# Regrouping the projections, the attention and its filler in a hybrid encoder block

## The chip, the cores and the metric

The kernel runs on one core of a Trainium2 chip. The metric is the device time of one launch in microseconds (us), lower is better. The kernel before takes 1700.06 us, the median of three runs (1698.44 to 1700.27).

## The reference

One residual block on x of 1024 rows (T) by 1024 channels. A normed x is multiplied by one wide input matrix, whose columns feed three token mixers and three merge gates. Then follow one output projection and a ConvGLU channel mixer.

```python
h = _rmsnorm(x, norm_mix_g); z = h @ w_in
(hq, hf, hi, hg, fq, fk, fv, ff, mq, gate_logits) = split(z)
y_a = _hgrn2_mixer(hq, hf, hi, hg, ...)      # gated linear recurrence, 4 heads, 128 x 128 state
y_b = _fox_mixer(fq, fk, fv, ff, ...)        # forgetting attention, 8 heads of 64, causal
y_c = _memory_mixer(mq, mem_kv, ...)         # cross-attention into 256 memory tokens, 4 heads of 128
gates = sigmoid(gate_logits)                 # 3 x 1024 channels
merged = sum(gates[b] * (y_b @ w_br[b]) for the three branches)
x = x + merged @ w_out
x = x + conv_glu_ffn(_rmsnorm(x, norm_ffn_g))

# inside _fox_mixer, for each block of 128 queries lo:hi
s = (q[lo:hi] @ k[:hi].T) * scale + Fc[lo:hi] - Fc[:hi]       # Fc: running sum of log-forget
p = softmax(where(causal, s, -inf)); out = p @ v[:hi]
```

## The kernel before

Every large product is done in three parts. Each fp32 operand is split into a rounded high part (ScalarE cast, L166) and the rest (VectorE subtraction, L174), and `mm3` (L160 to L162) issues high x high, high x low and low x high into one accumulation bank. On the profile these are the three lines with most of TensorE's time.

The instructions are not issued in the order of the program's text alone. A scheduler places them on each engine's queue by a simulated time and by priority; `ahead(gen, AHEAD)` raises the priority of a generator's steps, `weave` alternates the steps of several generators in given proportions, and `tc.issue_after(ins)` puts an order on one engine: what is built inside stands behind `ins` on its queue, with no wait for its end. `held` (in the recurrence) uses this to spread filler.

The stages, in order of time:

- The start loads x, makes high and low parts of x^T (`uh`, `ul`, in eight chunks of 128 channels) and does the first two gates and the memory tokens' keys and values.
- The dense stage (`dense_unit`) does the four chunks of the cross-attention's queries and ten gate chunks in pairs, each pair with seven block products in place of eight (Winograd's form of Strassen's scheme): 7 x 4 x 3 matmuls for two chunks of 128 output channels. Its weights come on GpSimd's DMA queue. A chunk done directly (`cm_chunk`) takes 8 k-chunks x 2 halves x 3 matmuls of 512 columns.
- `fox_values` (values and forget logits) and `fox_proj(0)` make the attention's inputs token by token: in `token_major` the stationary operand is a 128-token block of `uh` or `ul`, and 256 (or 264) columns of weights move through. The cross-attention (`memory`) runs between them.
- The attention goes by pairs of heads. `fox_prep(p)` transposes a pair's normed queries and keys and makes `kh`, `kl`, `qa`. `fox_attn(p, i)` goes through one head: two query blocks get logits (L924, L925), bias and row maximum (L930), exp (L940), reciprocal (L941) and scaling on GpSimd (L942); then the scaled blocks are transposed (L953 to L956), split, and multiplied with the values (L965, L966), 256 columns at a time. The next two query blocks follow.
- Between those steps TensorE gets other work, the filler: in a pair's first head the next pair's projection, in its second head three gate chunks (`gates_early`); in the last pair the recurrence's values (`hgrn_values`) and one gate. `fox_prep(p + 1)` stands between the two heads of pair p, behind the last logits.
- The recurrence (`hgrn_prep`, `hgrn_mix`), with the next head's preparation as filler, then the three branch projections, the output projection, the ConvGLU up products (the same seven-product scheme) and the down products.

Names that the text uses: `Vf` holds the attention's values and later the recurrence's; `rt` and `rx` are the norm of a row, by token and spread; `gd`, `mqd`, `ybd`, `ycd` are DRAM scratch; `raw`, `wh`, `wl` are a weight tile and its two parts.

Of the kernel before, what the change touches and what calls it, by code (L numbers as in the profile page):

```python
# [14 lines left out]
P = 128  # L15
# [13 lines left out]
NCOVER, NPAIR = 2, 10  # L29
NDULL = 8  # L30
NFOX = [0, 3, 0, 3, 0, 3, 1]
# [3 lines left out]
assert 2 + NCOVER + NPAIR + sum(NFOX) == len(ORDER) and len(_dense) % 2 == 0  # L35
# [3 lines left out]
FOX_STEPS, HGRN_STEPS, MEM_STEPS = 28, 14, 7  # L39
AHEAD = 300  # L40
FOX_LATE = 0.2
# [68 lines left out]
def tile_block(ctx: ExitStack, tc: tile.TileContext, xT, memT, x_rows, mem_rows, vec, fbias, mats, hmask, w_first, w_cm, w_hi, w_fqk, w_fv,  # L110
# [77 lines left out]
    def weights(src, shape, raw=None, hl=None, parts=1):  # L188
# [4 lines left out]
        if hl is None:  # L193
            hl = [wp.tile([P, 4 * 264], F32R, tag=t, name=t, bufs=3) for t in ("wh", "wl")]
# [227 lines left out]
    def first_weights(k):  # L422
        k0, k1 = WFIRST[k]
        if k % 4 == 0:
            gw[k // 4] = [wp.tile([P, 4 * 264], F32R, tag=t, name=t, bufs=3) for t in ("wh", "wl")]
        sl = slice((k0 % 4) * 256, (k1 - 1) % 4 * 256 + 256)
        split(S, gw[k // 4][0][:, sl], gw[k // 4][1][:, sl], wg[k // 4][:, sl])
# [124 lines left out]
    def product(ps, op, b, first):  # L552
        wh, wl = op
        for k in range(4):
            ks = slice(k * P, (k + 1) * P)
            bh, bl = block(b, k)
            mm3(ps, wh[:, ks], wl[:, ks], bh, bl, first and k == 0, k == 3, not first)

    class Dense:
# [16 lines left out]
        def operand(self, src):  # L576
            if self.half is None:
                self.half = [wp.tile([P, 4 * 264], F32R, tag=t, name=t, bufs=3) for t in ("wh", "wl")]
# [125 lines left out]
    def token_major(src, ncol, evac):  # L704

        with tc.issue_after(late["load"].ins):
            w = [weights(src[q], (4, ncol)) for q in range(2)]
        for tb in range(8):
            ps = ps_proj()[:, :ncol]
            tsl = slice(tb * P, (tb + 1) * P)  # L710
            for k in range(KC):
                wh, wl = w[k // 4]
                mm3(ps, uh[k][:, tsl], ul[k][:, tsl], wh[:, k % 4, :], wl[:, k % 4, :], k == 0, k == KC - 1)
# [130 lines left out]
    def fox_proj(p):  # L844

        fox_z[p] = [None, None]

        def evac(tb, ps):
            n, b = tb // 4, tb % 4
            if b == 0:  # L850
                fox_z[p][n] = pq.tile([P, 4, 256], F32, tag="z", name=f"z{p}_{n}", bufs=2)
            z = fox_z[p][n]
            S.activation(z[:, b, :], ps, AF.Copy, scale=rt[:, tb:tb + 1])
            if b == 3:
                zz = z.rearrange("p b (h d) -> p (b h) d", d=64)
                sq = pools["pf"].tile([P, 16, 64], F32, tag="pt", name="fsq", bufs=4) if p else \
                    pm.tile([P, 16, 64], F32, tag="fsq", name="fsq")
                r = cp.tile([P, 16], F32, tag="fr", name="fr", bufs=2)
                S.activation(sq, zz, AF.Square)
                V.reduce_sum(r, sq, axis=AX.X)  # L860
                rstd_small(r, r, 64)
                V.tensor_mul(zz, zz, r.unsqueeze(2).to_broadcast([P, 16, 64]))

        yield from token_major(w_fqk[p], 256, evac)

    def fox_prep(p, after=None):
# [3 lines left out]
        for n in range(2):  # L870
            sl = slice(n * HB, (n + 1) * HB)
            z = fox_z[p][n]
            for what in range(2):
                gc = col(C_FK) if what == 0 else fqs
                ptr = ps_tr()
                with tc.issue_after(after.ins) if after is not None else nullcontext():
                    for b in range(4):
                        PE.transpose(ptr[:, b * P:(b + 1) * P], z[:, b, what * P:(what + 1) * P], ident)
# [13 lines left out]
        fox_sets[p] = [kh, kl, qa, None]  # L892
# [7 lines left out]

    def fox_attn(p, i):
        kh, kl, qa, _ = fox_sets[p]
# [7 lines left out]
        for tp in range(4):  # L910
            pts = []
            for j in range(2):
                tb = 2 * tp + j
                ns = (tb + 1) * P
                tsl = slice(tb * P, (tb + 1) * P)
                pt = pf.tile([P, T], F32, tag="pt", name="pt", bufs=4)
# [4 lines left out]
                for s0 in range(0, ns, HB):  # L921
# [3 lines left out]
                    fox_sets[p][3] = PE.matmul(ps[:, :w], qa[i][:, tsl], kl[i][:, s0:s0 + w], start=False, stop=True)  # L925
# [14 lines left out]
                S.activation(pt[:, :ns], pt[:, :ns], AF.Exp, bias=st[:, 2:3], accum_out=st[:, 3:4])  # L940
                V.reciprocal(st[:, 3:4], st[:, 3:4])  # L941
                G.tensor_scalar(pt[:, :ns], pt[:, :ns], st[:, 3:4], 0.0, ALU.mult, ALU.add)  # L942
                pts.append(pt)
                yield
            po = ps_po()
            for sp in range(tp + 1):
                ptr = ps_tr()
                w = 384 if sp == tp else 512
                for jj in range(2):
                    sb = 2 * sp + jj  # L950
                    ssl = slice(sb * P, (sb + 1) * P)
                    if sb <= 2 * tp:
                        PE.transpose(ptr[:, jj * 256:jj * 256 + P], pts[0][:, ssl], ident)  # L953
                        PE.transpose(ptr[:, jj * 256 + P:jj * 256 + 256], pts[1][:, ssl], ident)
                    else:
                        PE.transpose(ptr[:, 256:384], pts[1][:, ssl], ident)  # L956
                ph = pf.tile([P, HB], F32R, tag="ph", name="ph", bufs=2)
                pl = pf.tile([P, HB], F32R, tag="pl", name="pl", bufs=2)
                split(S, ph[:, :w], pl[:, :w], ptr[:, :w])
                for jj in range(2):  # L960
                    sb = 2 * sp + jj
                    last = sb == 2 * tp + 1
                    o = po[:, P:256] if last else po[:, 0:256]
                    src = slice(256, 384) if last else slice(jj * 256, jj * 256 + 256)
                    PE.matmul(o, vhl[:, sb, :], ph[:, src], start=(sb == 0), stop=False)  # L965
                    PE.matmul(o, vhl[:, sb, :], pl[:, src], start=False, stop=last)  # L966
# [848 lines left out]
```

## Time and profile before

| | |
|---|---|
| runs | 1698.44, 1700.06, 1700.27 us, median 1700.06 |
| profiled execution | 1700.23 us, its span 1698.4 us |
| TensorE matmul busy | 1691.0 us, 8957 instructions |
| VectorE, ScalarE, GpSimd busy | 1150.8, 800.9, 324.6 us |
| TensorE clock granted, mean | 0.999 |
| DMA moved | 227.16 MB, mean 134 GB/s |

A row of an instruction group reads: line, engine, operation, tiles written and read, shape, count, then busy time in us, mean ns of one, and idle time before them with what ended it. A row of a window reads: start and end, then the busy us of each engine with its count of instructions, granted clock, share of the DMA engines, GB/s. In a list by time the first two numbers are start and duration in us. Ends of matmuls are modelled and overlap the next one.

### The profile page before, as it was taken

To read this page: it belongs to the slowest core of one execution; us is meant where nothing else is said; L and a number is where in the kernel's file an instruction comes from. 1 tells how busy PE (TensorE), PEld (TensorE's weight loads), DVE (VectorE), ACT (ScalarE), POOL (GpSimd) and SP (SyncE) were. 2 spreads that over 40 slices of the span, in tenths; PEclk is the share of its full clock that TensorE was granted. 3 is DMA by queue.
4 is the path that set the end of the run, shared out by engine and by line. 5 is a ranking of instruction groups with operands and counts; after the bars stand their busy time and mean duration, and the time that the engine had idled before them with its cause. 6 is when DMAs were issued, how large, how long until landed. Compare 5 with 4: busy or idle time off the path is not lost.

```text
span 1698.4 us, 24291 instructions
## 1 busy us (share of the span) xinstructions
PE 1691.0 (100%) x8957; PEld 1452.4 (86%) x8957; DVE 1150.8 (68%) x2057; ACT 800.9 (47%) x1428; POOL 324.6 (19%) x420
## 2 busy tenths in 40 slices
PE   9999999999999999999999999999999999999999
PEld 7888899989898998888888888888888888888887
DVE  6966455666666664886856845987878888775654
ACT  6734455545454553775631333644434444533432
POOL 0200032543433331544310000311111111100000
PEclk9999999999999999999999999999999999999999
DMA  9443232221212111110346542566544344494772
GB/s 367 157 161 106 88 139 68 77 92 51 94 59 77 63 46 57 67 32 13 106 127 209 167 186 100 165 174 169 158 139 138 118 149 143 172 363 145 251 269 87
DMA packets 83062, 227.16 MB, mean 134 GB/s; under 512 B 9712, under 2 KB 12408, under 8 KB 82816
## 3 DMA queue, kind: packets, MB, share of 16 engines
q1 hardware_dynamic: 64320, 160.54, 26.8%
q0 software_dynamic: 18048, 64.50, 13.2%
q8 instruction: 70, 1.15, 0.3%
q10 hardware_dynamic: 576, 0.59, 0.1%
q14 instruction: 48, 0.39, 0.1%
HBM read 180.72 MB, written 67.93 MB: 146 GB/s over the span
## 4 chain that ended last, share of the span: by engine, by line
PE 99%; DVE 0%; ACT 0%; DMA 0%; issue 0%; ACTq 0%; DVEq 0%
PE pp L160 21%; PE pp L162 21%; PE pp L161 21%; PE lg L160 4%; PE lg L162 4%; PE lg L161 4%; PE tr L162 3%; PE tr L161 3%; PE tr L160 3%; PE po L966 1%; PE lg L925 1%; PE lg L924 1%; PE po L965 1%; PE po L160 1%; PE po L161 1%; PE po L162 1%
## 5 line engine op out<-in xcount | busy, mean ns | idle before, releaser
L160 PE MATMUL pp<-uh,wh 128*128 128x512 f32 x412 | 163.3, 396 | 0.0
L161 PE MATMUL pp<-ul,wh 128*128 128x512 f32 x412 | 162.9, 395 | 0.0
L162 PE MATMUL pp<-uh,wl 128*128 128x512 f32 x412 | 162.5, 394 | 0.0
L161 PE MATMUL pp<-wl,uh 128*128 128x256 f32 (+1 forms) x512 | 146.3, 286 | 0.0
L162 PE MATMUL pp<-wh,ul 128*128 128x256 f32 (+1 forms) x512 | 146.1, 286 | 0.0
L160 PE MATMUL pp<-wh,uh 128*128 128x256 f32 (+1 forms) x512 | 145.6, 286 | 0.0
L166 ACT CAST wh<-s 128x512 fp32r<-128x512 f32 x110 | 66.5, 621 | 131.6 <-PE pp L161 55.1
L166 ACT CAST wh<-raw 128x1024 fp32r<-128x1024 f32 (+2 forms) x76 | 67.6, 890 | 100.6 <-PE pp L161 86.2
L166 ACT CAST wh<-rw 128x512 fp32r<-128x512 f32 x87 | 53.2, 619 | 108.1 <-PE pp L161 70.2
L160 PEld LDWEIGHTS pp<-wh,uh 128*128 128x128 f32 x512 | 97.3, 190 | 1.2
L161 PEld LDWEIGHTS pp<-wl,uh 128*128 128x128 f32 x512 | 97.4, 190 | 1.0
L162 PEld LDWEIGHTS pp<-wh,ul 128*128 128x128 f32 x512 | 97.4, 190 | 0.9
L1457 POOL DMA_DIRECT2D rw<-in_w_up x44 | 24.1, 555 | 372.4 <-DVE wl L1350 171.3
L166 ACT CAST dwh<-wr 128x1024 fp32r<-128x1024 f32 (+1 forms) x41 | 40.2, 980 | 115.8 <-PE tr L161 40.0
L162 PEld LDWEIGHTS pp<-uh,wl 128*128 128x128 f32 x412 | 77.5, 188 | 15.1
L174 DVE TENSOR_TENSOR wl<-raw,wh 128x1024 fp32r<-128x1024 f32 (+2 forms) x75 | 78.0, 1040 | 17.8 <-ACT wh L166 17.6
L160 PEld LDWEIGHTS pp<-uh,wh 128*128 128x128 f32 x412 | 77.5, 188 | 14.6
L161 PEld LDWEIGHTS pp<-ul,wh 128*128 128x128 f32 x412 | 77.5, 188 | 14.5
L940 ACT ACTIVATE pt<-pt,st 128x128 f32<-128x128 f32 (+3 forms) x64 | 49.7, 777 | 41.7 <-DVE st L937 33.9
L174 DVE TENSOR_TENSOR dwl<-wr,dwh 128x1024 fp32r<-128x1024 f32 (+1 forms) x41 | 46.3, 1129 | 31.7 <-ACT dwh L166 31.7
L942 POOL TENSOR_SCALAR pt<-pt,st 128x128 f32<-128x128 f32 (+3 forms) x64 | 49.1, 767 | 78.4 <-DVE st L941 64.1
L1350 DVE TENSOR_TENSOR wl<-rw,wh 128x512 fp32r<-128x512 f32 x69 | 47.7, 704 | 22.7 <-PE pp L162 18.2
(500 smaller groups left out, 5123.2 us busy)
## 6 DMA issues: line engine op xcount, KB each, us to landing
rw<-in_w_up POOLq DMA_DIRECT2D x44, 512.0 KB, 4.7
sd<-in_w_dn POOLq DMA_DIRECT2D x30, 512.0 KB, 6.0
br<-yd SPq DMA_DIRECT2D x30, 512.0 KB, 5.0
raw<-in_w_cm SPq DMA_DIRECT2D x24, 512.0 KB, 3.4
gd<-gt SPq DMA_DIRECT2D x48, 256.0 KB, 2.0
gt<-gd SPq DMA_DIRECT2D x48, 256.0 KB, 2.7
yd<-fc SPq DMA_DIRECT2D x44, 256.0 KB, 2.2
wr<-sd SPq DMA_DIRECT2D x20, 512.0 KB, 4.5
```

Source lines behind the costliest of these rows:

```text
L160: PE.matmul(ps, lh, rh, start=first, stop=False, skip_group_check=more)
L161: PE.matmul(ps, lh, rl, start=False, stop=False, skip_group_check=more)
L162: return PE.matmul(ps, ll, rh, start=False, stop=last, skip_group_check=more)
L166: return S.copy(out, in_)
L174: return (sub or V).tensor_sub(l, src, h.bitcast(F32))
L924: PE.matmul(ps[:, :w], qa[i][:, tsl], kh[i][:, s0:s0 + w], start=True, stop=False)
L925: fox_sets[p][3] = PE.matmul(ps[:, :w], qa[i][:, tsl], kl[i][:, s0:s0 + w], start=False, stop=True)
L940: S.activation(pt[:, :ns], pt[:, :ns], AF.Exp, bias=st[:, 2:3], accum_out=st[:, 3:4])
L942: G.tensor_scalar(pt[:, :ns], pt[:, :ns], st[:, 3:4], 0.0, ALU.mult, ALU.add)
L965: PE.matmul(o, vhl[:, sb, :], ph[:, src], start=(sb == 0), stop=False)
L1350: late["split"] = V.tensor_sub(l, src, h.bitcast(F32))
L1457: late["raw"] = G.dma_start(raw[:, 2 * i:2 * i + 2, :], src[:, 2 * i:2 * i + 2, :])
```

## The change

- Four more gate chunks go to the dense stage (`NPAIR` 10 to 14); the attention keeps six (`NFOX`).
- The queries and keys of pairs 2 and 3 are one 512-column weight matrix, and so are the recurrence's values (`w_late`). `token_major` then takes 512 moving columns. The results are stored to DRAM (`zd`, `hid`) and read back: queries and keys by `fox_load`, which then applies the norm, and values into `Vf` after the attention.
- `fox_attn` works on four query blocks at a time: four softmaxes, then transposes and value products of up to 512 columns (fewer where the causal mask ends a block).
- `fox_prep(p + 1)` is woven into the second head of pair p. It and all filler go through `paced`: each step stands behind the attention step `FOX_LAG` = 4 before it on TensorE's queue. Pair 1's projection is split: its weights and three of its eight blocks come ahead of the first head. The filler of each head is listed by hand (`fill`). The recurrence's first preparation is paced behind the last attention steps, and the last head's output is written after its third step.
- There are four weight buffers (`WIDE`) where three were, and the per-partition scratch for GpSimd's DMA descriptors is 2048 bytes.
- The cross-attention's result is loaded one tile at a time during the recurrence's branch, each load behind a small GpSimd instruction that reads a gate.
- At the start of the ConvGLU the first raw weights come on SyncE's queue, the eviction of one bank, the norm's row and the last operand's split are ordered later.

```diff
-NCOVER, NPAIR = 2, 10
+NCOVER, NPAIR = 2, 14
-NFOX = [0, 3, 0, 3, 0, 3, 1]
+NFOX, NMID, NREST = 6, (2, 3), (4, 4, 4, 4, 2)
-FOX_STEPS, HGRN_STEPS, MEM_STEPS = 28, 14, 7
+FOX_STEPS, HGRN_STEPS, MEM_STEPS = 22, 14, 7
-FOX_LATE = 0.2
+FOX_LAG = 4
+WIDE = 4
...
+    def token_major(src, ncol, evac, lead=False):
         with tc.issue_after(late["load"].ins):
-            w = [weights(src[q], (4, ncol)) for q in range(2)]
+            per = 2 if ncol == HB else 4
+            w = [weights(src[q], (per, ncol)) for q in range(KC // per)]
+        if lead:
+            yield
...
+    def fox_proj_late():
+        def evac(tb, ps):
+            t = gate_tile()
+            S.activation(t, ps, AF.Copy, scale=rt[:, tb:tb + 1])
+            SP.dma_start(zd[tb], t)
+        yield from token_major(w_late[0], HB, evac)
+
+    def fox_load(p):
+        cs = slice((p - 2) * 256, (p - 1) * 256)
+        for n in range(2):
+            z = fox_tile(p, n)
+            SP.dma_start(z, zd[4 * n:4 * n + 4, :, cs].rearrange("b p c -> p b c"))
+            fox_norm(z)
+            yield
...
+    def paced(gen, lag):
+        while True:
+            with tc.issue_after(at[-lag].ins) if len(at) >= lag else nullcontext():
+                try:
+                    next(gen)
+                except StopIteration:
+                    return
+            yield
...
-        for tp in range(4):
+        for g in range(2):
             pts = []
-            for j in range(2):
-                tb = 2 * tp + j
+            for tb in range(4 * g, 4 * g + 4):
...
             po = ps_po()
-            for sp in range(tp + 1):
+            for sb in range(4 * g + 4):
                 ptr = ps_tr()
+                first = max(sb - 4 * g, 0)
+                for j in range(first, 4):
+                    PE.transpose(ptr[:, j * P:(j + 1) * P], pts[j][:, sb * P:(sb + 1) * P], ident)
...
+                c = slice(first * P, HB)
+                split(S, ph[:, c], pl[:, c], ptr[:, c])
+                PE.matmul(po[:, c], vhl[:, sb, :], ph[:, c], start=sb == 0, stop=False)
+                at.append(PE.matmul(po[:, c], vhl[:, sb, :], pl[:, c], start=False, stop=sb == 4 * g + 3))
...
-    for p in range(3):
-        weave((ahead(fox_attn(p, 0), AHEAD), FOX_STEPS), (fox_proj(p + 1), 8))
-        fox_prep(p + 1, fox_sets[p][3])
-        weave((ahead(fox_attn(p, 1), AHEAD), FOX_STEPS), (gates_early(NFOX[2 * p + 1]), 2 * NFOX[2 * p + 1], FOX_LATE))
+    first = fox_prep(0)
+    run_all(islice(first, 2))
+    for _ in range(3):
+        next(pair1)
+        next(first, None)
...
+    fill = [(pair1, 5), (chain(islice(gates, NMID[0]), islice(late_proj, NMID[1])), sum(NMID)),
+            (islice(late_proj, 8 - NMID[1]), 8 - NMID[1])]
+    fill += [(islice(rest, n), n) for n in NREST]
+    for h in range(7):
+        p = h // 2
+        more = [(paced(fox_prep(p + 1), FOX_LAG), 4, 0.15)] if h % 2 and p < 3 else []
+        if h == 3:
+            run_all(fox_load(2))
+        if h == 4:
+            more = [(fox_load(3), 2, 0.2)]
+        gen, n = fill[h]
+        weave((ahead(fox_attn(p, h % 2), AHEAD), FOX_STEPS), (paced(gen, FOX_LAG), n), *more)
...
+    weave((ahead(fox_attn(3, 1), AHEAD), FOX_STEPS), (paced(fill[7][0], FOX_LAG), 2 * fill[7][1]))
     run_all(values)
+    for tb in range(8):
+        SP.dma_start(Vf[:, tb, :], hid[tb])
...
-    run_all(hgrn_prep(0))
+    tail = hgrn_prep(0)
+    for i, lag in enumerate((12, 9, 6, 3, 1, 1, 1)):
+        run_all(paced(islice(tail, 1), lag))
+        if i == 2:
+            fox_out(gate_tile()[:64, :], *late.pop("tail"))
...
-    for c in range(4):
-        for t, d in zip(yc, ycd):
-            with tc.issue_after(state["norm"].ins):
-                G.dma_start(t[c], d[:, c, :].bitcast(F32R))
-    run_all(branch(0, yh, yl))
+    for i, _ in enumerate(first_branch):
+        if i % 3 and i < 12:
+            p, c = i % 3 - 1, i // 3
+            mark = G.tensor_scalar(warm, late["gates"][:, 0:1], 1.0, 0.0, ALU.mult, ALU.add)
+            with tc.issue_after(mark.ins):
+                G.dma_start(yc[p][c], ycd[p][:, c, :].bitcast(F32R))
...
-            late["raw"] = G.dma_start(raw[:, 2 * i:2 * i + 2, :], src[:, 2 * i:2 * i + 2, :])
+            with tc.issue_after(late["pow"].ins) if after else nullcontext():
+                late["raw"] = (SP if begun else G).dma_start(raw[:, 2 * i:2 * i + 2, :], src[:, 2 * i:2 * i + 2, :])
...
-    nc = bacc.Bacc("TRN2", target_bir_lowering=False, num_devices=1)
+    nc = bacc.Bacc("TRN2", target_bir_lowering=False, num_devices=1, dynamic_dma_scratch_size=2048)
```

More of the change, by code (lines that the diff above doesn't have):

```diff
@@ L1474, in unit @@
             o4 = operand(sum_of(4, s2, a12))
-            o5 = operand(sum_of(3, a11, a21))
-        product(y, o4, "B22", False)
+            with tc.issue_after(after.ins) if after else nullcontext():
+                s3 = sum_of(3, a11, a21)
+            o5 = operand(s3)
+        ins = product(y, o4, "B22", False)
+        if begun:
+            e2 = late["e2"]
+            with tc.issue_after(ins.ins):
+                spread(r2, rt2)
         put(0, 1, y, e2)
@@ L1498, in families @@
             with ExitStack() as order:
+                if name == "T4":
+                    with tc.issue_after(late["last"].ins):
+                        late["last operand"] = late["last operand"]()
+                    late["o7"] = late["cast"]
                 if after:
```

156 lines of the change are left out of this document (80 added, 76 removed).

## The prediction

> **What bounds the kernel.** I read the page first, then the chain that ended last, then busy time by stage, then single TensorE instructions in order of time.
>
> ```profile
> span 1698.4 us, 24291 instructions
> PE 1691.0 (100%) x8957; PEld 1452.4 (86%) x8957; DVE 1150.8 (68%) x2057; ACT 800.9 (47%) x1428; POOL 324.6 (19%) x420
> PEclk9999999999999999999999999999999999999999
> ...
> PE 99%; DVE 0%; ACT 0%; DMA 0%; issue 0%; ACTq 0%; DVEq 0%
> PE pp L160 21%; PE pp L162 21%; PE pp L161 21%; PE lg L160 4%; PE lg L162 4%; PE lg L161 4%; PE tr L162 3%; PE tr L161 3%; PE tr L160 3%; PE po L966 1%; PE lg L925 1%; PE lg L924 1%; PE po L965 1%; PE po L160 1%; PE po L161 1%; PE po L162 1%
> ```
>
> The chain is TensorE from end to end, at full clock, and most of it are the three products of mm3 (L160 to L162). But a recorded matmul overlaps the next one, so "100%" may hide slack. What an instruction costs is its step: the start of the next one less its own start.
>
> ```profile
> 207.31 0.28 PE L160 MATMUL pp<-wh,uh 128*128 128x256 f32 x1
> 207.43 0.28 PE L161 MATMUL pp<-wl,uh 128*128 128x256 f32 x1
> 207.55 0.28 PE L162 MATMUL pp<-wh,ul 128*128 128x256 f32 x1
> 207.67 0.28 PE L160 MATMUL pp<-wh,uh 128*128 128x256 f32 x1
> ...
> 44.94 0.39 PE L160 MATMUL pp<-wh,umh 128*128 128x512 f32 x1
> 45.16 0.39 PE L161 MATMUL pp<-wl,umh 128*128 128x512 f32 x1
> 45.39 0.39 PE L162 MATMUL pp<-wh,uml 128*128 128x512 f32 x1
> 45.62 0.39 PE L160 MATMUL tr<-wh,umh 128*128 128x512 f32 x1
> ```
>
> The columns are start, duration, engine and line. A product 256 columns wide steps by 0.36/3 = 0.120 us, one 512 wide by 0.68/3 = 0.227 us. The second group has the same operand order as the first (activations stationary, weights moving), so it is the price of what the change widens. Two narrow ones cost 0.240, a wide one 0.227: 13 ns an instruction is all that width saves.
>
> ```profile
> core 0: us, PE busy (x) PEld busy (x) DVE busy (x) ACT busy (x) POOL busy (x), PEclk, DMA share, GB/s
> 327.00:681.00 354.00, 354.00 (x2338) 323.26 (x2337) 216.87 (x649) 180.85 (x355) 121.18 (x169) 1.00 0.19 65
> 700.00:825.00 125.00, 125.00 (x755) 106.84 (x754) 97.44 (x161) 83.10 (x201) 55.87 (x47) 1.00 0.13 43
> 1100.00:1490.00 390.00, 390.00 (x1723) 322.92 (x1722) 311.61 (x461) 168.08 (x251) 54.24 (x88) 1.00 0.52 151
> ```
>
> By stage: 327 to 681 us is the forgetting attention with its filler, 700 to 825 most of the recurrence, 1100 to 1490 the ConvGLU up products. The last has 1723 products in 390 us, 0.226 us each, which is the bare step: no slack there, although VectorE is 80% busy. In the attention stage VectorE is 61% busy. So the kernel takes what TensorE's instruction list takes; a change gains by shortening that list, and loses where TensorE starts to wait.
>
> **Four gates in the dense stage.** A gate chunk done directly issues 8 k x 2 halves x 3 = 48 products of 512 columns. A pair in the dense stage issues 7 block products x 4 k x 3 = 84 for two chunks, against 96. Two more pairs: 24 products fewer, 24 x 0.226 = 5.4 us. The added operand sums, casts and subtractions lie on VectorE and ScalarE, and the loads on POOL's queue, at the rate that this stage has already:
>
> ```profile
> 100.00:140.00 40.00, 40.00 (x178) 33.14 (x177) 20.32 (x32) 14.18 (x26) 2.87 (x6) 1.00 0.29 105
> rw<-in_w_pair POOLq DMA_DIRECT2D x12, 512.0 KB, 5.5
> ```
>
> TensorE full, VectorE at 51%, and two loads of 5.5 us to landing for a unit of 84 x 0.226 = 19 us. I take no cost beside; uncovered, one load would be 5.5 us. What leaves attention is 4 x 48 x 0.226 = 43.4 us of filler.
>
> **Wide projections.** Query/key pairs 2 and 3 and the recurrence's values change from 256-wide to 512-wide products. Count:
>
> ```profile
> L160 PE MATMUL pp<-wh,uh 128*128 128x256 f32 x448 | 127.1, 285 | 0.0
> ```
>
> 448 on each of three lines is 64 for the first half of the attention values, 4 x 64 for the four pairs, 2 x 64 for the recurrence's values. Half of the pairs' and all of the latter, 256 a line and 768 in all, become 384: 768 x 0.120 - 384 x 0.227 = 92.2 - 87.2 = 5.0 us. [...]
>
> The results go through DRAM: 16 stores of 256 KB, four loads of 512 KB (with a norm behind) and eight of 256 KB, all on SP's queue. The nearest rows, a spilled tile of the memory branch and a norm:
>
> ```profile
> mqd<-gt SPq DMA_DIRECT2D x8, 256.0 KB, 2.0
> mqf<-mqd SPq DMA_DIRECT2D x4, 512.0 KB, 4.2
> L179 POOL TENSOR_TENSOR fr<-fr,mhalf 128x16 f32<-128x16 f32 x6 | 17.5, 2910 | 2.9 <-DVE st L941 2.8
> ```
>
> (The third row is of the attention stage's groups.) Store, load and power take 2.0 + 4.2 + 2.9 = 9 us before the multiply. Pair 2's loads stand at the head of head 3, its operands are needed in head 4; a head is some 37 us long (295 / 8, below). Behind a store that waits for ScalarE, SP holds up the weights of the next filler and the head's bias row; DMA is at 19% in this stage. Zero, and at worst one exposed 9 us. The same store and load for the recurrence's values end under the first head's preparation.
>
> **Wide probability-times-value products.** Groups of four query blocks replace groups of two, with the same columns:
>
> ```profile
> 645.48 0.28 PE L965 MATMUL po<-ph,vhl 128*128 128x256 f32 x1
> 645.59 0.28 PE L966 MATMUL po<-pl,vhl 128*128 128x256 f32 x1
> 645.71 0.22 PE L965 MATMUL po<-ph,vhl 128*128 128x128 f32 x1
> 645.77 0.28 PE L966 MATMUL po<-pl,vhl 128*128 128x128 f32 x1
> 645.89 0.45 PE L162 MATMUL pp<-uh,wl 128*128 128x512 f32 x1
> ...
> 649.82 0.33 PE L924 MATMUL lg<-kh,qa 128*128 128x384 f32 x1
> 650.00 0.34 PE L925 MATMUL lg<-kl,qa 128*128 128x384 f32 x1
> 650.17 0.40 PE L162 MATMUL pp<-uh,wl 128*128 128x512 f32 x1
> ```
>
> A high/low couple costs 0.23 us at 256 columns, 0.18 at 128, 0.35 at 384 (the bias product of that width), 0.45 at 512. Before, a head has 16 + 4 couples: 16 x 0.23 + 4 x 0.18 = 4.4 us. After: 6 x 0.45 + 2 x (0.35 + 0.23 + 0.18) = 4.2. Eight heads save about 1.5 us. Transposes stay 36 a head.
>
> **What holds the rest.** The holds are orders on TensorE's queue alone: a filler step stands behind the attention step four before it, so nothing waits for a semaphore, but TensorE passes filler only in these places. Preparing the next pair inside the odd heads moves 8 transposes a half and their ScalarE, VectorE and GpSimd work off the boundary between heads. Before, no boundary shows idle time, so that gains nothing. What it must cover is the softmax. Here is the last block of the last head (last logits, then exp, reciprocal, scaling):
>
> ```profile
> 654.08 0.39 PE L925 MATMUL lg<-kl,qa 128*128 128x512 f32 x1
> 658.65 1.15 ACT L940 ACTIVATE pt<-pt,st 128x1024 f32<-128x1024 f32 x1 [1.71 <-DVE st L937]
> 659.92 0.16 DVE L941 RECIPROCAL st<-st 128x1 f32<-128x1 f32 x1 [1.37 <-ACT pt L940]
> 660.25 1.12 POOL L942 TENSOR_SCALAR pt<-pt,st 128x1024 f32<-128x1024 f32 x1 [6.18 <-PE tr L956]
> ```
>
> From the end of the logits (654.47) to the scaled block (661.37) is 6.9 us, in which TensorE needs other work. After the change a head has two such places. Heads 1 to 6 carry 4 or 5 filler steps of 24 x 0.227 = 5.4 us, 22 to 27 us for two waits of at most 6.9; the last head has 2 steps and the recurrence's first preparation (6 x 8 x 3 x 0.227 = 32.7 us). The thinnest is head 0: five steps of 24 x 0.120 = 14.4 us against 13.8. VectorE is no limit: 8 evictions and 4 weight splits leave (0.69 and 1.23 us by the rows below), 216.9 - 10.4 = 206.5 us in a stage of 354 - 43.4 - 5.0 - 1.5 - 8.6 (three blocks moved ahead of it) = 295 us, 70%, against 80% with a full TensorE further on.
>
> ```profile
> L464 DVE TENSOR_TENSOR gt<-pp,rx 128x512 f32<-128x512 f32 x20 | 13.8, 689 | 20.3 <-PE pp L162 20.3
> L174 DVE TENSOR_TENSOR wl<-raw,wh 128x1024 fp32r<-128x1024 f32 x22 | 27.1, 1232 | 8.4 <-ACT wh L166 8.4
> ```
>
> I add 1 us for new waits, most of it in head 0; bounds 0 and, if head 0 covered neither wait, 13.8.
>
> **Later edits.** The cross-attention's result is now loaded behind marks on POOL's queue, one tile at a time through the first 11 of 16 half chunks of the recurrence's branch, instead of eight at once (a mark waits for a loaded gate, and behind it are only these loads):
>
> ```profile
> ycl<-ycld POOLq DMA_DIRECT2D x4, 512.0 KB, 9.6
> 1062.00:1100.00 38.00, 37.82 (x183) 31.44 (x182) 35.49 (x57) 26.79 (x46) 12.76 (x15) 1.00 0.56 170
> ```
>
> The last load issues at about 11/16 of 16 x 12 x 0.227 = 43.6 us, which leaves 13.6 us for 9.6: free, at worst 9.6 late. At the start of the ConvGLU (the second row) the eviction, the norm's row and the last operand change order, and the first raw load moves to SP's queue; 0.2 us of idle time is all there is to win, and I take 0, within 1 us either way. A fourth weight buffer only lets loads start earlier. The smaller descriptor scratch leaves POOL's transfers as they are: they come singly or in pairs with a landing of 5 to 10 us.
>
> **Sum.** -5.4 - 5.0 - 1.5 + 1.0 = -10.9 us. The profiled execution took 1700.23 (span 1698.44 and 1.8 around it), 0.17 over the median of the runs, 1700.06. So 1689.2 on the median.
>
> **Rivals.** (a) *Wide products save only their half*: a wide one costs as much per column as the narrow one (0.240), so only the gates and 1.5 us of the value products pay, and waits take 1: 1700.1 - 5.9 = 1694.2. Against it stands the 0.227 step of the same operand order. [...] 7%.
> (b) *The filler that left is replaced by waits*, about 12 us over the eight heads, 1.5 us a head: about 1700. For it: 43.4 of the filler's microseconds are gone and the holds forbid using the rest early. Against: what remains is twice what the waits ask. 7%.
> (c) *Slower: the second group of each head is uncovered from the exponential on.* The hold keeps a filler step behind the attention step four back, so filler may be spent while VectorE reduces the four large blocks, and TensorE then stands through exp, reciprocal and scaling, 1.15 + 0.16 + 1.12 = 2.4 us, in eight heads: 19.4 us, 1700.1 - 11.9 + 19.4 = 1707.6. It ends slower from 1.9 us a head. For it: the block's 6.9 us above are 30% longer than a filler step of 5.4. Against: the next head's first logits have buffers of their own and can run there. 13%. [...]
>
> **How the numbers follow.** My forecast has 73%. The lowest of the bounds is 1700.1 - 11.9 - 1 (start of the ConvGLU) and about 2 us if interleaving transposes with wide products costs less than now: 1685. Upwards the range takes in (a), (b) and an exposed transfer of 9 us, to 1699; (c) and half of (b) are left out. This kernel's measurement can tell about 0.2%, 3.4 us. Faster: the forecast and (a), 80%. Within: (b), 7%. Slower: (c), 13%.
>
> **What would show it.** Right: attention (from its first logits to the first product of the recurrence) some 55 to 60 us shorter, the dense stage 38 us longer; 192 256-wide products a line instead of 448, and 128 512-wide ones more; the chain still 99% TensorE, recurrence and ConvGLU as long as now. Wrong: idle TensorE, or steps much over 0.227 us, between a head's last logits and its transposes; a chain through exp (L940's successor) or through loads of the spilled tiles; a granted clock below 1.00 in the attention stage.

## The result and the profile after

The changed kernel takes 1729.82 us, the median of four runs (1729.52 to 1732.43), against 1700.16 for the kernel before beside it (four runs, 1698.44 to 1700.27). The ratio is 1.0182, with a 95% interval of 1.0166 to 1.0197. The forecast was 1689.2.

The page of the changed kernel: the span, the matmuls, the chain, and one group of mm3.

```profile
span 1728.1 us, 23292 instructions
PE 1698.3 (98%) x8421; PEld 1425.0 (82%) x8421; DVE 1156.9 (67%) x2089; ACT 802.9 (46%) x1436; POOL 336.6 (19%) x430
...
PE 94%; DVE 2%; issue 1%; DMA 1%; POOL 1%; ACT 1%; ACTq 0%; POOLq 0%; DVEq 0%; SPq 0%
...
L161 PE MATMUL pp<-wh,uh 128*128 128x256 f32 (+2 forms) x384 | 124.5, 324 | 0.0
```

TensorE has 536 matmuls fewer (8957 to 8421), as the change intends: 24 of the gates, 384 of the widening, 128 of the value products. And yet the span is 29.7 us longer. The chain shows why: TensorE held 99% of it, now 94%, and the rest belongs to engines that TensorE waits for.

To place the loss I take every TensorE instruction's step (start to next start) and subtract the bare step of its shape from the prediction. What is left over, summed, I call *lost time*. It is 22.0 us over the whole kernel before and 64.2 after, 42.2 more; 29.7 of those lengthen the span, so 12.5 us of work were saved, where the sum had 11.9. By place: in the eight attention heads 0.6 us before and 40.3 after; at the start of the ConvGLU 0.7 and 4.7; the rest moved by under 2 us in all.

Busy time in the eight heads of the changed kernel, from each head's first logits to the next head's (columns as in the prediction's windows):

```profile
364.00:384.00 20.00, 16.24 (x96) 13.60 (x94) 15.01 (x59) 10.92 (x24) 15.46 (x21) 0.83 0.00 1
384.00:428.00 44.00, 43.72 (x254) 37.69 (x253) 28.47 (x91) 24.01 (x48) 20.36 (x25) 1.00 0.24 84
428.00:462.00 34.00, 31.21 (x161) 25.03 (x160) 19.40 (x72) 17.39 (x35) 11.72 (x20) 1.00 0.17 55
462.00:516.00 54.00, 50.25 (x244) 41.79 (x243) 35.54 (x95) 28.84 (x54) 21.66 (x26) 0.94 0.35 120
516.00:550.00 34.00, 31.73 (x162) 25.31 (x160) 25.75 (x77) 19.01 (x38) 17.96 (x21) 1.00 0.17 58
550.00:599.00 49.00, 45.26 (x215) 36.22 (x215) 28.30 (x89) 22.17 (x46) 14.94 (x24) 0.97 0.27 89
599.00:633.00 34.00, 32.13 (x160) 26.07 (x159) 18.25 (x63) 15.98 (x32) 10.44 (x18) 0.95 0.11 37
633.00:667.00 34.00, 32.77 (x169) 26.70 (x168) 19.01 (x77) 17.32 (x37) 10.63 (x17) 1.00 0.28 92
```

Before, the same stage read 354.00 busy of 354.00 at clock 1.00. Now TensorE is visibly idle for 19.7 of 303 us, in every head. Lost time by head is 7.4, 1.0, 5.0, 7.1, 4.4, 8.1, 4.9 and 2.6 us. It is about twice the idle time because the modelled end of a matmul covers the first 0.1 to 0.2 us of a gap (a 512-wide product is recorded with 0.39 us and steps by 0.227, a 256-wide one with 0.28 and 0.120), and because the clock fell: 1 less the clock column, times the length, is 9.8 us over these rows (3.4 + 3.2 + 1.5 + 1.7).

What TensorE waited for between 364 and 667 us (total, times, longest; the four largest of ten):

```profile
PE po L1002 <- DVE pl L175: 6.5, 8, 2.3
PE po L1001 <- ACT ph L167: 3.2, 5, 1.4
PE tr L996 <- POOL pt L987: 2.4, 2, 2.0
PE lg L969 <- DVE st L975: 2.3, 5, 0.6
```

The same question of the kernel before, 327 to 681 us, has no answer at all. Over half of the waiting isn't for the softmax (L987, L975, L986) but behind it, where the transposed probabilities are split into `ph` and `pl`. One such gap in order of time:

```profile
501.38 1.15 ACT L985 ACTIVATE pt<-pt,st 128x1024 f32<-128x1024 f32 x1
501.43 2.92 POOL L180 TENSOR_TENSOR fr<-fr,mhalf 128x16 f32<-128x16 f32 x1
...
502.53 1.03 ACT L167 CAST wh<-raw 128x1024 fp32r<-128x1024 f32 x1
503.58 0.75 ACT L167 CAST ph<-tr 128x384 fp32r<-128x384 f32 x2
503.59 1.23 DVE L175 TENSOR_TENSOR wl<-raw,wh 128x1024 fp32r<-128x1024 f32 x1
504.12 0.44 PE L1001 MATMUL po<-ph,vhl 128*128 128x384 f32 x1 [1.41 <-ACT ph L167]
504.73 1.63 DVE L859 TENSOR_TENSOR z<-z,fr 128x1024 f32<-128x1024 f32 x1
506.29 0.88 DVE L175 TENSOR_TENSOR pl<-tr,ph 128x384 fp32r<-128x384 f32 x2
506.89 0.69 PE L1002 MATMUL po<-pl,vhl 128*128 128x384 f32 x1 [2.34 <-DVE pl L175]
```

TensorE asks for one high part and one low part. ScalarE first finishes an exponential and a weight cast, VectorE first a weight's low part and the multiply of the next pair's norm. Each is about 1 to 1.6 us; between 501.6 and 509.2 us no filler product starts on TensorE.

And the clock, in pieces of the heads above (the third and fourth row are the halves of the second):

```profile
376.00:382.00 6.00, 4.72 (x16) 3.83 (x17) 4.52 (x19) 2.38 (x6) 3.98 (x7) 0.50 0.00 0
502.00:508.00 6.00, 2.25 (x9) 1.42 (x8) 4.58 (x7) 3.02 (x7) 5.75 (x5) 0.75 0.42 144
502.00:505.00 3.00, 1.14 (x5) 0.39 (x3) 2.41 (x5) 2.84 (x6) 2.91 (x2) 1.00 0.13 38
505.00:508.00 3.00, 1.11 (x4) 1.03 (x5) 2.17 (x3) 0.17 (x1) 2.84 (x4) 0.50 0.71 250
508.00:512.00 4.00, 4.00 (x15) 3.43 (x14) 2.40 (x4) 2.04 (x4) 0.49 (x1) 0.52 0.41 138
```

In 502 to 508 TensorE worked 2.25 of 6 us. The clock falls to one half in the middle, behind the first of the two waits and at the start of the second, and TensorE, busy again from 508 us, still has 0.52.

### The profile page after: what moved, and what is told of

It reads as the page before. It is cut to its first block, busy times and chain, and to the rows that moved or that the text cites. A ratio compares the mean times of both kernels' runs of the same rounds, so it can differ in the third digit from the quotient of the medians.

```text
span 1728.1 us, 23292 instructions
## 1 busy us (share of the span) xinstructions
PE 1698.3 (98%) x8421; PEld 1425.0 (82%) x8421; DVE 1156.9 (67%) x2089; ACT 802.9 (46%) x1436; POOL 336.6 (19%) x430
## 4 chain that ended last, share of the span: by engine, by line
PE 94%; DVE 2%; issue 1%; DMA 1%; POOL 1%; ACT 1%; ACTq 0%; POOLq 0%; DVEq 0%; SPq 0%
PE pp L161 20%; PE pp L162 20%; PE pp L163 20%; PE lg L161 5%; PE lg L163 5%; PE lg L162 5%; PE tr L162 3%; PE tr L163 3%; PE tr L161 3%; PE tr L996 2%; PE po L1002 1%; PE po L161 1%; PE po L162 1%; PE po L163 1%; PE lg L1211 1%
## 5 line engine op out<-in xcount | busy, mean ns | idle before, releaser
L161 PE MATMUL pp<-uh,wh 128*128 128x512 f32 x356 | 142.0, 399 | 0.0
L163 PE MATMUL pp<-uh,wl 128*128 128x512 f32 x356 | 141.2, 397 | 0.0
L161 PE MATMUL pp<-wh,uh 128*128 128x256 f32 (+2 forms) x384 | 124.5, 324 | 0.0
L162 PE MATMUL pp<-wl,uh 128*128 128x256 f32 (+2 forms) x384 | 124.5, 324 | 0.0
L163 PE MATMUL pp<-wh,ul 128*128 128x256 f32 (+2 forms) x384 | 124.1, 323 | 0.0
L167 ACT CAST wh<-rw 128x512 fp32r<-128x512 f32 x93 | 56.8, 619 | 112.9 <-PE pp L162 64.2
L175 DVE TENSOR_TENSOR pl<-tr,ph 128x512 fp32r<-128x512 f32 (+1 forms) x96 | 51.7, 550 | 42.1 <-ACT ph L167 37.7
L167 ACT CAST ph<-tr 128x512 fp32r<-128x512 f32 (+1 forms) x96 | 44.4, 478 | 73.9 <-PE tr L996 68.1
L163 PEld LDWEIGHTS pp<-wh,ul 128*128 128x128 f32 x384 | 73.3, 191 | 5.4
L162 PEld LDWEIGHTS pp<-wl,uh 128*128 128x128 f32 x384 | 73.4, 191 | 5.0
L161 PEld LDWEIGHTS pp<-wh,uh 128*128 128x128 f32 x384 | 73.4, 191 | 4.7
L985 ACT ACTIVATE pt<-pt,st 128x128 f32<-128x128 f32 (+3 forms) x64 | 49.6, 776 | 30.9 <-DVE st L982 22.1
L1411 DVE TENSOR_TENSOR wl<-rw,wh 128x512 fp32r<-128x512 f32 x69 | 46.6, 687 | 21.8 <-PE pp L163 18.5
```

Of the source, the lines that this page charges most:

```text
L161: PE.matmul(ps, lh, rh, start=first, stop=False, skip_group_check=more)
L162: PE.matmul(ps, lh, rl, start=False, stop=False, skip_group_check=more)
L163: return PE.matmul(ps, ll, rh, start=False, stop=last, skip_group_check=more)
L167: return S.copy(out, in_)
L175: return (sub or V).tensor_sub(l, src, h.bitcast(F32))
L985: S.activation(pt, pt, AF.Exp, bias=st[:, 2:3], accum_out=st[:, 3:4])
```

## The experiments

The question: is it the filler that left, the hold that keeps filler back, or one of the other parts (groups of four, the next pair inside the head, wide products, scratch)? "Before" in the ratios is the kernel before on the same chip; lost time means that of the eight heads, by head in brackets where it matters. All ratios have 95% intervals.

**Filler.** Four gates back to the attention, all else as after:

```diff
-NCOVER, NPAIR = 2, 14
+NCOVER, NPAIR = 2, 10
-NFOX, NMID, NREST = 6, (2, 3), (4, 4, 4, 4, 2)
+NFOX, NMID, NREST = 10, (2, 3), (6, 6, 6, 6, 2)
```

> The changed kernel with the four gates back in the attention (ten there, ten in the dense stage), two more halves of filler in each of heads 3 to 6. T1, too little filler: the 40 us of waits in the attention go to under 5, 1730 + 5.4 - 35 = 1700 us. T2, the hold, and T3, groups of four: the waits stay for the most part, 1725 to 1735 us.

1714.75 us, ratio 1.0087 [1.0057, 1.0116]; lost 20.5 us (7.7, 1.0, 3.3, 1.1, 4.8, 0.4, 1.5, 0.8). Half the loss goes, and 15 us with it, although the dense stage's 5.4 us are given up again. Heads 0 to 2, whose lists didn't change, lose what they lost.

The same move alone, made in the kernel before:

```diff
-NCOVER, NPAIR = 2, 10
+NCOVER, NPAIR = 2, 14
-NFOX = [0, 3, 0, 3, 0, 3, 1]
+NFOX = [0, 2, 0, 2, 0, 1, 1]
```

> The kernel before with only the four gates moved to the dense stage (attention fillers 2, 2, 1, 1 gates in place of 3, 3, 3, 1). T1, too little filler: 1700 - 5.4 + 20 to 35 = 1715 to 1730 us. T2, the hold, and T3, groups of four: 1695 to 1700 us.

1716.3 us, 1.0096 [1.0067, 1.0125]; lost 16.6 us in the heads and about 6 at the start of the recurrence. Its windows for head 6 and for the recurrence's start:

```profile
606.00:635.00 29.00, 24.62 (x164) 22.19 (x163) 19.11 (x77) 17.36 (x39) 12.54 (x19) 0.88 0.11 35
669.00:725.00 56.00, 51.76 (x266) 42.68 (x265) 32.13 (x61) 31.28 (x61) 17.44 (x15) 0.97 0.17 54
```

So moving the gates saves 5.4 us and costs 22, with no other part of the change present. And two gates only, again in the kernel before:

```diff
-NCOVER, NPAIR = 2, 10
+NCOVER, NPAIR = 2, 12
-NFOX = [0, 3, 0, 3, 0, 3, 1]
+NFOX = [0, 2, 0, 3, 0, 2, 1]
```

> The kernel before with two gates moved to the dense stage in place of four (fillers 2, 3, 2, 1). If the kernel before has filler to spare: 1700 - 2.7 = 1697.5 us. If it has none: half of what four cost, 1708 us.

1719.16 us, 1.0114 [1.0099, 1.0129]; lost 14.5 us in the heads (head 3: 4.6, head 6: 8.2) and 7 at the recurrence's start. Not half of the four: the first two gates taken away already cost it all. The lists cut are those of heads 1 and 5, and heads 3 and 6 lose, so the shortage moves on to later heads. The kernel before has not even two gates of filler to spare.

More gates than the kernel before has in the attention, twelve and fourteen (the second with the values in brackets):

```diff
-NCOVER, NPAIR = 2, 14
+NCOVER, NPAIR = 2, 8                               # (6)
-NFOX, NMID, NREST = 6, (2, 3), (4, 4, 4, 4, 2)
+NFOX, NMID, NREST = 12, (2, 3), (7, 7, 7, 7, 2)    # (14; 8, 8, 8, 8, 2)
```

> The kernel after with six of the gates back in the attention, two more than the kernel before has there (NPAIR 8, NFOX 12, heads 3 to 6 with seven steps of filler each). The dense stage's seven-product form is lost for two more gates, 2.7 us. Theory F (the waits that stay with four gates back, 20.5 us, are still a lack of filler): they fall to 12 us or less, nearly all of it in head 0, whose filler isn't changed (7.7 us there); in all 1710 us. Theory K (what stays is the order on the queues of ScalarE and VectorE, whatever the filler): 20 us of waits, 1717.5 us.

> The same with eight gates back (NPAIR 6, NFOX 14, heads 3 to 6 with eight steps each): another 2.7 us in the dense stage. Theory F: no more than head 0's 8 us are left in the attention, 1709 us. Theory K: 20 us, 1720 us. If filler were a pure price, one microsecond of wait for one of filler, these two would both stand level with the kernel before plus what head 0 waits, 1708 us.

With 12: 1722.49 us, 1.0133 [1.0118, 1.0148]; lost 24.3 (6.8, 1.0, 5.0, 4.5, 3.5, 1.2, 2.2, 0.2). That fits neither theory: two gates more, and it lost more than with ten. With 14: 1718.63 us, 1.0111 [1.0094, 1.0127]; lost 16.0 (6.9, 0.9, 5.9, 0.3, 0.8, 0.3, 0.8, 0.2). With 14, heads 0, 2, 3, 4 and 5 read:

```profile
290.00:309.00 19.00, 15.62 (x90) 12.71 (x89) 14.45 (x59) 10.91 (x24) 14.45 (x21) 0.82 0.01 1
...
353.00:388.00 35.00, 32.80 (x161) 26.29 (x160) 19.65 (x73) 18.25 (x38) 12.05 (x20) 0.95 0.18 56
388.00:446.00 58.00, 58.00 (x290) 48.66 (x290) 37.66 (x96) 30.17 (x55) 22.17 (x25) 1.00 0.38 125
446.00:492.00 46.00, 45.91 (x233) 38.31 (x232) 31.72 (x89) 23.17 (x45) 20.36 (x22) 1.00 0.29 96
492.00:561.00 69.00, 69.00 (x339) 57.71 (x338) 33.88 (x90) 26.88 (x50) 13.18 (x22) 1.00 0.27 92
```

So the loss has two parts. Heads 3 to 7 lose 27.1 us after, 8.6 with four gates back, 11.6 with six, 2.4 with eight: more filler takes their loss away (with six the trend breaks, mostly in head 3; that stays unexplained). Heads 0 to 2, whose lists are the same in all four kernels, lose 12 to 14 us in each.

**The hold.** No hold, so filler comes when the scheduler likes:

```diff
-FOX_LAG = 4
+FOX_LAG = 10 ** 9
```

> The changed kernel without the hold on the filler and on the preparation inside the heads; the hold on the recurrence's first preparation stays. T2, the hold: 1730 - 35 = 1695 us. T1, too little filler, and T3, groups of four: no better, 1728 to 1745 us, since the filler is spent earlier.

1727.25 us, 1.0160 [1.0119, 1.0201], two runs 5 us apart; lost 35.1 us, but elsewhere: heads 0 to 4 at most 0.4 each, heads 5 to 7 15.1, 8.3 and 10.2. Head 0's first 20 us, then heads 5, 6 and 7:

```profile
364.00:384.00 20.00, 20.00 (x149) 19.06 (x148) 16.03 (x56) 13.87 (x28) 14.72 (x19) 1.00 0.00 1
...
592.00:620.00 28.00, 20.51 (x91) 15.40 (x90) 21.38 (x76) 18.21 (x38) 15.84 (x23) 0.76 0.31 109
620.00:641.00 21.00, 16.87 (x84) 12.25 (x84) 18.82 (x64) 13.58 (x29) 9.89 (x18) 0.92 0.14 42
641.00:675.00 34.00, 29.81 (x146) 23.58 (x144) 20.55 (x85) 17.54 (x38) 13.18 (x21) 0.90 0.20 69
```

In 20 us head 0 issues 149 matmuls where after issues 96. So the filler was there, and the hold kept it back. That is shown for head 0 (the longer list below); heads 1 and 2 lose almost nothing here either, but they also draw on later lists. For without the hold the early heads use what the late heads need, and heads 5 and 6 run with no filler at all. Gates back and no hold:

> The changed kernel with the four gates back in the attention and no hold on the filler. If the amount of filler counts and the hold only moves the waits about: heads 5 and 6, which ran dry without the hold, are covered, 1727 + 5.4 - 25 = 1707 us. If the hold is what makes scarce filler reach to the end: 1715 us or more.

1719.4 us, 1.0113 [1.0084, 1.0143]; lost 22.1 us, heads 0 to 5 at most 0.4 each, heads 6 and 7 9.2 and 10.9. The same picture; the filler lasts one head longer. A looser hold:

```diff
-FOX_LAG = 4
+FOX_LAG = 8
```

> The changed kernel with the hold loosened from four attention steps back to eight. If the hold of four puts the filler in the wrong places: heads 0 to 6 lose most of their 38 us of waits and the last heads still have filler, 1705 to 1715 us. If the amount alone counts: 1725 us or more.

1717.9 us, 1.0108 [1.0093, 1.0123]; lost 24.9 (3.0, 2.7, 2.6, 0.8, 10.2, 1.1, 4.3, 0.2). 12 us better than a distance of 4: heads 0 to 2 lose 8.3 us in place of 13.4, the others 16.6 in place of 27.1. With the same lists, head 3 goes from 7.1 to 0.8 us and head 5 from 8.1 to 1.1, while head 4 goes from 4.4 to 10.2. So the hold also has a share in the loss of heads 3 to 7, and the shares of hold and filler can't be told apart there. And a longer list for head 0 under the old hold, pair 1's eight blocks in place of five:

```diff
-    for _ in range(3):
-        next(pair1)
-        next(first, None)
+    run_all(first)
...
-    fill = [(pair1, 5), ...
+    fill = [(pair1, 8), ...
```

> The changed kernel with all eight blocks of pair 1's projection as filler of head 0, none ahead of it. If head 0 is short of filler: its 7.4 us of waits go, 1723 us. If its waits come from the queues of the other engines: 1729 us.

1729.4 us, 1.0175 [1.0145, 1.0204]; lost 39.7, head 0 still 6.9. Head 0 doesn't lack blocks; it may not use them. Here is head 0 with 8 blocks listed (it runs from 362.1 to 380.5 us), and its first 20 us with a distance of 8:

```profile
362.00:380.00 18.00, 15.15 (x82) 13.11 (x81) 15.60 (x63) 9.97 (x22) 11.94 (x22) 0.81 0.01 1
```

```profile
364.00:384.00 20.00, 18.10 (x131) 16.35 (x131) 16.47 (x65) 12.08 (x27) 15.35 (x22) 1.00 0.00 1
```

**The other parts.** Groups of two query blocks, as before, in the changed kernel, and the same with four gates back:

```diff
-        for g in range(2):
+        for tp in range(4):
...
-            for tb in range(4 * g, 4 * g + 4):
+            for tb in range(2 * tp, 2 * tp + 2):
...
```

> The changed kernel with groups of two query blocks (256-wide value products, four rotating buffers) as before, all else as changed. T3, groups of four: 1730 + 1.5 - 35 = 1696 us. T1, too little filler, and T2, the hold: the waits stay, 1725 to 1735 us.

> The changed kernel with the four gates back and groups of two query blocks. If groups of four raise what a head needs to cover: 1715 + 1.5 - 12 = 1704 us. If not: 1716 us.

1729.01 us, 1.0171 [1.0141, 1.02], lost 37.8; and 1722.36 us, 1.0131 [1.0101, 1.016], lost 23.4. Going back to groups of two doesn't help either kernel; with the gates back it is some 7 us slower, though the two intervals overlap. (A distance of four steps spans other steps when the groups are smaller, so these two runs change the hold a little too.) The other way round, groups of four alone in the kernel before (with the smaller scratch, for room):

```diff
-        for tp in range(4):
+        for g in range(2):
...
-            for j in range(2):
-                tb = 2 * tp + j
+            for tb in range(4 * g, 4 * g + 4):
...
```

> The kernel before with only groups of four query blocks (and the smaller scratch, which makes the room for their buffers). If groups of four raise what a head needs to cover: 1705 to 1715 us. If not: 1700 - 1.5 = 1698.5 us, plus what the smaller scratch costs by the run beside.

1719.97 us, 1.0117 [1.0087, 1.0146]: 8.5 us over the kernel before with the smaller scratch alone (below), 4.5 lost in the heads and about 9 at the attention's end. In the old order the larger group costs something; in the new one it doesn't show.

The next pair's operands between the heads again, behind the last value product of the head before (the kernel before made them earlier, behind its last logits):

```diff
-        more = [(paced(fox_prep(p + 1), FOX_LAG), 4, 0.15)] if h % 2 and p < 3 else []
+        if h % 2 == 0 and h:
+            run_all(paced(fox_prep(p), 1))
+        more = []
```

> The changed kernel with the next pair's operands made between the heads again, behind the last step of the head before. If making them inside the head crowds VectorE's and ScalarE's queues: heads 1, 3 and 5 lose their 16 us of waits and some come back between the heads, 1718 to 1724 us. If it does not: 1730 to 1740 us.

1743.51 us, 1.0258 [1.0228, 1.0287]; lost 53.8. The largest wait, in the same form as above:

```profile
PE lg L969 <- DVE qa L918: 12.4, 6, 4.9
```

Making them inside the head is worth 14 us in this kernel against this place. Against the place that the kernel before had, no run here prices it.

The norms' inverse square root on GpSimd taken out of the attention's operands (2.92 us at 501.43 us in the gap above), once as after, once with the gates back:

```diff
-        rstd_small(r, r, 64)
+        V.tensor_scalar(r, r, 1.0 / 64, EPS, ALU.mult, ALU.add)
```

> The changed kernel without GpSimd's inverse square root in the attention's norms (eight of 2.9 us; queries and keys are scaled with the mean square instead). Theory Q, the queues: this power stands ahead of the scaling of probabilities on GpSimd, and TensorE's transposes behind that; the waits of 40 us fall by 8 to 15, 1715 to 1722 us. Rival, it is hidden: 1728 to 1731 us.

> The same without the inverse square root, with the four gates back. Theory Q: of the 20 us of waits 8 to 12 go, above all in heads 0 and 4, 1703 to 1707 us. Rival: 1715 us.

1728.99 us, 1.0172 [1.0143, 1.0202], lost 37.0; and 1716.41 us, 1.0098 [1.0069, 1.0127], lost 20.9. The power isn't it.

The recurrence's values 512 wide, straight into `Vf`, in the kernel before (with four weight buffers, scratch of 7680 bytes and one gate moved from head 6 to head 5):

```diff
-NFOX = [0, 3, 0, 3, 0, 3, 1]
+NFOX = [0, 3, 0, 3, 0, 4, 0]
...
-        for pc in range(2):
-            def evac(tb, ps, pc=pc):
-                S.activation(Vf[:, tb, pc * 256:(pc + 1) * 256], ps, AF.Copy, scale=rt[:, tb:tb + 1])
-            yield from token_major(w_hi[pc], 256, evac)
+        def evac(tb, ps):
+            S.activation(Vf[:, tb, :], ps, AF.Copy, scale=rt[:, tb:tb + 1])
+        yield from token_major(w_hi, HB, evac)
```

> The kernel before with only the recurrence's values as 512-wide products (384 of 256 columns become 192), four weight buffers, a scratch of 7680 bytes to make their room, and the last attention gate moved one head ahead. The width's price holds: 384 x 0.120 - 192 x 0.227 = 2.5 us less, 1697.5 us. Rival, a wide one costs two narrow ones: 1700 us.

1713.35 us, 1.0079 [1.0064, 1.0094]; lost 9.1 us in the heads (head 6: 7.5) and 7.8 at the start of the ConvGLU. Head 6, which gave up its gate, waits; the loss at the ConvGLU's start isn't explained, and the price of width can't be read from this run.

**Scratch and the ConvGLU's start.** The smaller descriptor scratch alone in the kernel before:

```diff
-    nc = bacc.Bacc("TRN2", target_bir_lowering=False, num_devices=1)
+    nc = bacc.Bacc("TRN2", target_bir_lowering=False, num_devices=1, dynamic_dma_scratch_size=2048)
```

> The kernel before with only the smaller descriptor scratch for GpSimd's DMAs. Theory S, GpSimd's two slow subtractions at the start of the ConvGLU come from the smaller scratch: 1700 + 4 = 1704 us, and these two take near 4.9 us each in place of 1.5. Rival, they come from the new order there: 1700 us, 1.5 us each.

1711.47 us, 1.0065 [1.0043, 1.0088]. Nothing in the attention (lost 0.6, as before). The cost lies in one place, in the branch projections. The window, the loads that begin there, and TensorE's wait:

```profile
890.00:925.00 35.00, 26.94 (x113) 21.66 (x112) 17.29 (x26) 3.53 (x5) 1.06 (x2) 0.90 0.90 329
```

```profile
894.50 6.31 SPq L1336 DMA_DIRECT2D x<-in_xT  x8
```

```profile
913.94 0.77 PE L160 MATMUL pp<-yh,wh 128*128 128x512 f32 x1 [8.06 <-DVE gt L1293]
```

In the kernel before the same eight loads of x^T start at 977 us, and this window reads 35.00 busy of 35.00. With the smaller scratch, this run's only edit, they start 83 us earlier; DMA rises from 74% to 90%, and a gate that is being read back comes late (VectorE waits 11.2 us for it). What lets them start earlier isn't shown. In the changed kernel these loads start at 1002 us, behind the branch projections as in the kernel before, and this loss doesn't appear. The two subtractions on GpSimd at the ConvGLU's start take 1.5 us each here, as before, so the scratch isn't what slows them in the changed kernel (next).

Last, gates back, a distance of 8, and at the ConvGLU's start all subtractions of `B21l` on VectorE:

```diff
-                    sub = G if name == "B21" and k > 1 else None
+                    sub = None
```

> The changed kernel with the four gates back, the hold at eight steps, and at the start of the ConvGLU all subtractions of the third family on VectorE instead of two on GpSimd. Amount and placing together: attention waits under 8 us (20 with the hold of four), the ConvGLU's start without its 4 us: 1715 - 12 - 4 = 1699 us. If the hold is no cause: 1711 us.

1714.63 us, 1.0086 [1.0069, 1.0103]; lost 21.3 in the heads, so the looser hold that helped with six gates does nothing with ten; and at the ConvGLU's start 2.1 us in place of 4.7. The subtractions there: on GpSimd in the kernel before (two in one row), on GpSimd in the changed kernel (with the shortest, median and longest in ns), the engines' busy time around these, and on VectorE in this one:

```profile
1075.13 2.98 POOL L174 TENSOR_TENSOR B21l<-x,B21h 128x512 fp32r<-128x512 f32 x2 [0.23 <-ACT B21h L166]
```

```profile
1101.56 9.71 POOL L175 TENSOR_TENSOR B21l<-x,B21h 128x512 fp32r<-128x512 f32 x2 [1.55 <-ACT B21h L167]
L175 POOL TENSOR_TENSOR B21l<-x,B21h x2: 1271/4871/8471, 1101.6 to 1110.0; 128x512 fp32r<-128x512 f32 x2
```

```profile
1101.00:1111.00 10.00, 6.68 (x32) 4.57 (x30) 9.12 (x19) 6.22 (x12) 9.44 (x2) 1.00 0.34 123
```

```profile
L175 DVE TENSOR_TENSOR B21l<-x,B21h x4: 677/678/679, 1090.5 to 1092.3; 128x512 fp32r<-128x512 f32 x4
```

One takes 1.3 to 1.7 us before, and 0.68 on VectorE. After, the two differ: the first takes 8.47 us, and the second, which starts at 1110.0 us, 1.27. TensorE waits for them 2.8 us in the changed kernel and with four gates back, 2.5 with a distance of 8 alone, and not at all in this run. No kernel of these beats the kernel before; the nearest is the scratch alone.

## Why the prediction was wrong

*What it got right.* The count and the price of the shortened list. 12.5 us of work went, against 11.9 (5.4 + 5.0 + 1.5). The dense stage grew by the 38 us named (the first product of the attention's values starts at 205.2 us, then at 243.2). A 512-wide product of the widened projections steps by (438.39 - 437.71) / 3 = 0.227 us:

```profile
437.71 0.39 PE L161 MATMUL pp<-wh,uh 128*128 128x512 f32 x1
437.94 0.39 PE L162 MATMUL pp<-wl,uh 128*128 128x512 f32 x1
438.16 0.39 PE L163 MATMUL pp<-wh,ul 128*128 128x512 f32 x1
438.39 0.39 PE L161 MATMUL pp<-wh,uh 128*128 128x512 f32 x1
```

So rival (a) falls. The spills, the spread loads of the cross-attention's result and the fourth buffer cost TensorE nothing that its waits show.

*The step that failed* is "What holds the rest", the term "I add 1 us for new waits", with its bounds 0 to 13.8. It measured 39.7 us. So the attention, from its first logits to the first product of the recurrence, became 22.6 us shorter (326.7 to 700.9 us, then 364.3 to 715.9) and not 55 to 60. Four things were wrong in this step.

1. "22 to 27 us for two waits of at most 6.9." The 6.9 us is the softmax of one block, taken where TensorE had enough to do. The splits behind it were left out, and they are the largest waits above. A head really left without filler shows the whole: with no hold, head 6 lasts 21.0 us and loses 8.3, so its own TensorE work is under 13, while the chain through ScalarE, VectorE and GpSimd takes the 21.
2. The filler of a head was counted as if any of it could fill any hole. The hold forbids that: head 0 had 14.4 us listed and issued 5.6 us of it inside the head. The prediction named "head 0" as the thinnest and bounded it by list length; the longer list (eight blocks) changed nothing, taking the hold away did. Heads 0 to 2 lose 12 to 14 us this way (for heads 1 and 2 it is argued, not isolated), and the looser hold shows a share in heads 3 and 5 too.
3. "VectorE is no limit", with 70%. True of the mean (189.74 of 303, 63%), but a mean says nothing of a queue: in the gap shown VectorE is busy 4.58 of 6 us, on work that isn't the one awaited.
4. The sum has no term for the clock; "a granted clock below 1.00 in the attention stage" stands only among the signs of a wrong forecast. The clock fell to one half though no wait in the attention is longer than 2.34 us; some 9.8 us.

The missing filler itself was dismissed in rival (b): heads 3 to 7 lose 27.1 us and get 18.5 back with four gates, 24.7 with eight. The looser hold alone gives the same heads 10.5 back, so the two causes overlap there and their shares don't add up. The line "what remains is twice what the waits ask" compared a list with one latency. Rival (c) had the sign and the kind (groups uncovered from the exponential on, because the hold ties filler to an order) and 13% of the chance, but 19.4 us where it was 39.7, and only the second group of each head.

The ConvGLU's start, "I take 0, within 1 us either way", cost 4.0 us: one of GpSimd's subtractions took 8.47 us, beside the reordered work on VectorE (busy 9.70 of 9.70 us). Moving them to VectorE took 2.6 us of it away; that run also has the gates back and the looser hold, but each of these alone leaves TensorE's wait for GpSimd as it was (2.8 and 2.5 us).

*What stays open.* How the loss of heads 3 to 7 divides between hold and filler; why six gates back lose more than four; why in the kernel before two gates cost as much as four; and what a hold loose in heads 0 to 2 and tight later, with ten or more gates, would give. The last wasn't tried.

## What to carry to other kernels

Work that fills a dependent chain's holes is a budget of its own: before moving it to where it is cheaper, measure what the chain takes with none of it (here 21 us a head, against 13 of its own work), and see whether the stage has any left over; a stage that is 100% busy with no wait may stand exactly at the edge. An order that ties filler to the chain's own steps withholds it just when the chain stalls, and taking the order away spends it too early: the waits move, and most of their sum stays (40.3 us, then 35.1); the distance between the two did better (24.9). Try each part of a combined change alone: here the place of one was worth 14 us, and one that looked like bookkeeping (a smaller scratch) cost 11 in the kernel before.

## What the runs showed of the hardware

The clock fell under short waits: it was one half from 505.0 to 511.8 us. In the 3 us before it fell TensorE had been busy 1.14 us, with one whole wait of 1.41 us, and no wait in the attention is longer than 2.34 us. Nor did it fall at every such wait: the one of 2.54 us at the ConvGLU's start left the clock at 1.00 (the row from 1101 to 1111 us). What decides isn't shown here.

One subtraction on GpSimd was slow beside a busy VectorE. The first, begun at 1101.56 us, took 8.47 us; VectorE worked without a break meanwhile (9.70 of the 9.70 us from 1100.4 to 1110.1), and over a dozen of its instructions began after the subtraction and ended before it. The second, from 1110.0 us on, took 1.27, with VectorE busy 0.12 of the 2 us from 1110 to 1112. In the kernel before, the two took 1.3 and 1.7 us, with VectorE busy 3.78 of 5 us (1074 to 1079). On VectorE the same subtraction took 0.68. Why the first was slow isn't shown.
